# Fewer identity products, and all six tiles turned ahead of the first sums

## The chip, the cores and the metric

The kernel runs on one core of a Trainium2 chip. The metric is the device time of one execution in microseconds (us); lower is better. The time before is 1680.26 us, the median of three runs (1679.79 to 1680.38).

## The reference

Two layers of a diffusion backbone over 512 latent tokens with a prefix of 256 context tokens, model width 1024. Each sub-layer is normalised, shifted and scaled by a modulation that comes from the conditioning vectors `c` (latent tokens) and `c_ctx` (context tokens). The part that matters here is the very beginning of layer 0:

```python
def _rms(x, gain, eps=1e-6):
    xf = x.astype(jnp.float32)
    y = xf * lax.rsqrt(jnp.mean(xf * xf, axis=-1, keepdims=True) + eps)
    return (y * gain.astype(jnp.float32)).astype(x.dtype)
...
sc = jax.nn.silu(c)
scc = jax.nn.silu(c_ctx)
...
m_lat = jnp.split((sc @ mod_w[l] + mod_b[l])[:, None, :], 6, axis=-1)
m_ctx = jnp.split((scc @ mod_w[l] + mod_b[l])[None, None, :], 6, axis=-1)
h_ctx = _modulate(_rms(x_ctx, norm_pre_mix[l]), m_ctx[0], m_ctx[1])
h_lat = _modulate(_rms(x_lat, norm_pre_mix[l]), m_lat[0], m_lat[1])
...
gq, gk, gv, gog, gz, aq, ak, av = _split(h @ w_in, EVEN_SIZES)
```

So 768 token rows are normalised, two of the six parts of the modulation (shift and scale) are matrix products of two vectors with 2048 columns of `mod_w`, and the result `h` goes into the input projection `even_w_in`. All that follows (gated linear attention, attention, feed-forward layers, the second layer) is untouched by the change.

## The kernel before, in words

The tokens are held as six tiles of 128 rows: 0 to 3 latent, 4 and 5 context. The order of work is 4, 5, 0, 1, 2, 3.

The program first runs `constants` (line 377): it builds an identity matrix, issues a number of identity products with `warm(n)` (n products of the identity with itself into a PSUM tile named `idle`, whose result nobody reads; TensorE takes each as two passes), loads the rows of small constants and turns them into columns with one transpose (`pt_rows`, copied to `col`), and from these columns makes `scT`, the activated conditioning vectors.

The first stage stands in `run` (from line 1919). Its steps:

- `fetch` loads the six tiles `xt` on the sync queue, and `loads(qd)` after it loads, quarter by quarter (`qd` 0 to 3), 256 columns of shift and of scale of `mod_w` (tiles `mraw`, nine buffers, two transfers of 256 KB each) and 256 rows of 288 columns of `even_w_in` (`zraw`).
- `turn(t)` normalises and transposes one tile. `mean_rstd` (line 697) squares the tile on ScalarE with a sum over the row (tile `junk`), then GpSimd adds epsilon (line 704) and raises to the power -0.5 (line 705, tile `rs`). VectorE scales the tile by it (line 1956); for the last three tiles this scaling is queued behind a stated earlier copy. TensorE transposes the eight blocks into a PSUM tile of two buffers (`mm_tile`), and a copy to `xT` (line 1961) empties it, on VectorE for the first, second and fifth tile turned, on ScalarE for the others.
- `sums(qd, ks)` multiplies `scT` with the columns of `mod_w`, four narrow products side by side, for the eight blocks of the contraction in two halves (`lo` and `hi`), into `mod_acc`.
- `weights(qd)` splits `zraw` into a rounded part and a remainder: a cast on ScalarE (line 803, `wH`), a difference on GpSimd (line 804, `wL`). It is queued behind the last two copies to `xT`.
- `cols(qd)` copies the sums (`modrows`, line 487), transposes them, adds the bias (`modcol`, line 499) and makes the scale columns `aff` (line 2003) on VectorE.
- `apply(qd, ...)` makes the two parts of `h` from `xT`: ScalarE line 2014, VectorE lines 2015 and 2016.
- `z(t0, qd, ...)` multiplies `h` with the split weights, three products for each block (PSUM tile `nat`).

A loop over the quarters then interleaves the projection of one quarter with the sums of the next. TensorE's instructions carry line 355 (products) and 358 (transposes).

`pin` (line 348) makes an instruction follow, on its own engine, the one traced before it, as long as `self.pinned` is set. All TensorE instructions go through it. The order on the other engines is settled by a planner that lays out the instructions by estimated readiness, unless an `issue_after` block names a predecessor. Semaphores between engines are set from the data.

Of the kernel before, what the change touches and what calls it, by code (L numbers as in the profile page):

```python
# [13 lines left out]
ALU = mybir.AluOpType  # L14
# [13 lines left out]
EPS = 1e-6  # L28
# [288 lines left out]
class Net:  # L317
# [59 lines left out]
    def constants(self):  # L377
        nc, I, cst = self.nc, self.I, self.cst
        self.ident = cst.tile([P, P], F32, name="ident")
        make_identity(nc, self.ident)  # L380
        self.idle = self.sc_tile("idle", 1)[:, :P]
        self.pinned = True
        self.warm(18)
        self.scT = cst.tile([P, KD, 32], F32, name="scT")
        self.neghalf = cst.tile([P, 1], F32, name="neghalf")
        nc.gpsimd.memset(self.neghalf, -0.5)
        self.one = cst.tile([P, 1], F32, name="one")
        nc.gpsimd.memset(self.one, 1.0)

        self.col = cst.tile([P, R_END], F32, name="col")  # L390
        self.modb = self.col[:, R_MB : R_MB + 96]
        self.col_rows(
            "rows", 0, P, (
                (R_C, I["c"].rearrange("o (k p) -> (o k) p", p=P), 8),
                (R_CC, I["c_ctx"].rearrange("(k p) -> k p", p=P), 8),
                (R_NPM, I["norm_pre_mix"].rearrange("l (k p) -> (l k) p", p=P), 16),
                (R_MB, I["mod_b"].rearrange("l (k p) -> (l k) p", p=P), 96),
            )
        )()
        self.pinned = False  # L400

        nc.gpsimd.memset(self.scT, 0.0)
        nc.scalar.activation(
            self.scT[:, :, 0:2].rearrange("p k r -> p r k"),
            self.col[:, R_C : R_C + 16].rearrange("p (r k) -> p r k", r=2),
            AF.Silu,
        )
        self.modcol, self.gates = {}, {}
# [288 lines left out]
    def mean_rstd(self, src):  # L697

        nc = self.nc
        junk = self.wp.tile([P, D], BF16, tag="mraw", bufs=2, name="junk")  # L700
        ms = self.sm.tile([P, 1], F32, tag="ss", name="ss")
        self.squared = nc.scalar.activation(junk, src, AF.Square, scale=1.0 / 32, accum_out=ms)
        rs = self.sm.tile([P, 1], F32, tag="rs1", name="rs")
        nc.gpsimd.tensor_scalar(ms, ms, EPS, None, op0=ALU.add)
        nc.gpsimd.tensor_tensor(rs, ms, self.neghalf, op=ALU.pow)
        return rs

    def pre_norm(self, pool, t, xt, A, B, h, xn):
# [406 lines left out]
    def even_mixer(self, h, mix, z):  # L1115
# [141 lines left out]

        self.pinned = True
        run("qk0 e m qk0 e e v0 qk0 e e m qk0 e e m v0 e e m m q v0 m m v0 m m kv q m q m q m m m m m m m m m m qk1 kv m")
        tp.release()  # L1260
        gp = self.open_pool("gla")
        run("c0 l0 kv m c0 kv c0 v1 qk1 c0 p p qk1 c0 l0 p qk1 l0 c0 g0 qk1 l0 p c1 p v1 l0 p v1 l0 c1 p v1 l0 c1 l1 g1 g0 c1 g0 r0 c1 l1 r0 g0 l1")
        self.tc.keep_in_program_order(nc.scalar.preload_act_table_set("exp_and_others"))
        run("r0 c1 g1 x l1 x g1 l1 x x l1 x l1 x")
        gp.release()
        mg.__exit__(None, None, None)
# [652 lines left out]
    def run(self):  # L1919
        nc, I, out = self.nc, self.I, self.out  # L1920
# [13 lines left out]
        order = (4, 5, 0, 1, 2, 3)  # L1934
# [4 lines left out]
        with self.pool("pre0") as pp:  # L1939
# [10 lines left out]
            def turn(t):  # L1950
                xt = xts.pop(t)
                rs = self.mean_rstd(xt)
                with ExitStack() as behind:
                    if len(emptied) > 2:
                        behind.enter_context(self.tc.issue_after(emptied[min(len(emptied) - 3, 1)].ins))
                    nc.vector.tensor_scalar(xt, xt, rs, None, op0=ALU.mult)
                pt = self.mm_tile(f"xT{t}")
                for k in range(KD):
                    self.tr(pt[:, k * P : (k + 1) * P], xt[:, k * P : (k + 1) * P], self.ident)
                copy = nc.vector.tensor_copy if len(emptied) in (0, 1, 4) else nc.scalar.copy  # L1960
                emptied.append(copy(xT[:, :, t * P : (t + 1) * P], pt.rearrange("p (k i) -> p k i", k=KD)))
# [7 lines left out]
            def loads(qd):  # L1969
                for k in range(0, KD, 2):  # L1970
                    u = pp.tile([P, 2, 2, 256], F32, tag="mraw", bufs=9, name=f"mraw00{qd}{k}")
                    for kk in range(2):
                        nc.sync.dma_start(
                            out=u[:, kk],
                            in_=I["mod_w"][0, (k + kk) * P : (k + kk + 1) * P, 0:2048].rearrange("p (m f) -> p m f", m=2)[
                                :, :, 256 * qd : 256 * qd + 256
                            ],
                        )
                    us[qd, k] = u
                src = w[256 * qd : 256 * qd + 256, 1536 : 1536 + 288].rearrange("(k p) m -> p k m", p=P)  # L1980
                zu.append(self.fetched(src, 2, 288, pp.tile([P, 576], F32, tag="zraw", bufs=4, name="zraw")))

            def sums(qd, ks):
                if ks[0] == 0:
                    accs[qd] = (self.sc_tile("mod_acc", qd) if qd < 2 else self.tr_tile("mod_acc"))[:, :P]
                for k in ks:
                    for j in range(4):
                        self.mm(
                            accs[qd][32 * j : 32 * j + 32, :],
                            self.scT[:, k, :],  # L1990
                            us[qd, k // 2 * 2][:, k % 2, j // 2, (j % 2) * P : (j % 2) * P + P],
                            start=(k == 0),
                            stop=(k == KD - 1),
                            tile_position=(0, 32 * j),
                        )
                if ks[-1] == KD - 1:
                    accs[qd] = self.mod_cols(0, accs[qd], P, [(m, r, 2 * qd, 2 * m, r, 2) for m in range(2) for r in range(2)])

            def cols(qd):
                accs[qd]()  # L2000
                ks = slice(2 * qd, 2 * qd + 2)
                gain = self.col[:, R_NPM + 2 * qd : R_NPM + 2 * qd + 2]
                nc.vector.scalar_tensor_tensor(
                    A[:, :, ks], self.mod_m(0, 1)[:, :, ks], 1.0, gain[:, None, :].to_broadcast([P, 2, 2]), op0=ALU.add, op1=ALU.mult
                )

            def apply(qd, r, t0, n):
                tok = slice(t0 * P, (t0 + n) * P)
                for k in range(2 * qd, 2 * qd + 2):
                    H, L = h.hl(k, tok)  # L2010
                    a, b = A[:, r, k : k + 1], B[:, r, k : k + 1]
                    x = xT[:, k, tok]
                    f = pp.tile([P, SEQ], F32, tag="xa", bufs=4, name="xa")[:, : n * P]
                    cast = nc.scalar.activation(H, x, AF.Identity, bias=b, scale=a)
                    nc.vector.tensor_scalar(f, x, a, b, op0=ALU.mult, op1=ALU.add)
                    self.mark = nc.vector.tensor_tensor(L, f, H.bitcast(F32), op=ALU.subtract)
                    self.latest = cast, self.mark

            def weights(qd):
                with self.behind():  # L2020
                    zu[qd] = zu[qd](vector=nc.gpsimd)
# [20 lines left out]
            fetch(*order)  # L2042
            for qd in range(4):
                loads(qd)
            for t, n in zip(order[:-1], (1, 18, 2, 3, 3)):
                turn(t)
                self.warm(n)
            sums(0, lo)
            turn(order[-1])
            self.warm(3)  # L2050
            sums(0, hi)
            self.latest = emptied[5], emptied[4]
            weights(0)
            self.warm(2)
            cols(0)
            self.warm(5)
            apply(0, 1, 4, 2)
            apply(0, 0, 0, 4)
            for qd in range(1, 4):
# [227 lines left out]
```

## Time and profile before

| | before |
|---|---|
| median of three runs | 1680.26 us |
| the profiled execution, its own time | 1680.16 us |
| its span | 1678.4 us |
| TensorE busy | 1649.9 us (98%) |
| VectorE busy | 1311.4 us (78%) |
| ScalarE busy | 915.6 us (55%) |
| GpSimd busy | 131.5 us (8%) |
| bytes moved by DMA | 204.79 MB |

PE is TensorE, PEld its weight loads, DVE is VectorE, ACT is ScalarE, POOL is GpSimd, SPq the sync engine's queue of transfers and ACTq ScalarE's. A row in order of time gives the start in us, the duration in us, the engine, the source line, the operation, what it writes and reads, the shapes, the number of merged instructions, and in brackets the idle time of the engine before it with what ended it. The chain of work is followed back from the last instruction, so that its rows add up to the span. In the rows of windows the last three columns are granted TensorE clock, DMA share and GB/s, and each engine has its busy time with the number of instructions. A transfer's row gives KB each and the median time from issue to landing.

### The profile page before, as it was taken

The numbers are of one execution on the slowest core, as the hardware profiler recorded it, in microseconds if no ns is written. First come the engines' busy times: TensorE is split into PE (matmuls) and PEld (weight loads), VectorE is DVE, ScalarE is ACT, GpSimd is POOL, SyncE is SP. The second block draws the span as 40 slices with busy tenths as digits, with TensorE's granted clock in tenths as the row PEclk, the third lists the DMA queues.
The fourth block names the chain that finished last, engine by engine and source line by source line (L and its number), as shares of the span: only waits on it lengthen the run. The fifth ranks groups of instructions, "written<-read, shape, count | busy, mean of one in ns | idle before, by whom it ended". The sixth has DMA issues, their size and how long they took to land.

```text
span 1678.4 us, 32622 instructions
## 1 busy us (share of the span) xinstructions
PE 1649.9 (98%) x13457; PEld 1486.4 (89%) x13457; DVE 1311.4 (78%) x2097; ACT 915.6 (55%) x1551; POOL 131.5 (8%) x139
## 2 busy tenths in 40 slices
PE   9999998999999999999999999999999999999998
PEld 8898987888999999998887788888888899999886
DVE  4889768876898989778668648778775599987887
ACT  4645557845544443445447536566564565555564
POOL 2004110001000000002101000000000100000310
PEclk9999999999999999999999999999999999999999
DMA  9651002164243446249516542111115334433973
GB/s 339 187 154 41 3 27 101 52 201 155 86 149 101 139 146 192 77 136 222 101 60 208 191 131 64 52 53 50 52 54 161 125 107 120 115 101 102 221 168 138
DMA packets 184736, 204.79 MB, mean 122 GB/s; under 512 B 7142, under 2 KB 141836, under 8 KB 184588
## 3 DMA queue, kind: packets, MB, share of 16 engines
q1 hardware_dynamic: 173996, 181.98, 34.7%
q0 software_dynamic: 9024, 17.30, 5.9%
q10 hardware_dynamic: 1568, 3.43, 0.6%
q8 instruction: 105, 1.72, 0.4%
q14 instruction: 43, 0.35, 0.1%
HBM read 193.23 MB, written 9.46 MB: 121 GB/s over the span
## 4 chain that ended last, share of the span: by engine, by line
PE 83%; DVE 8%; ACT 3%; DMA 3%; issue 2%; POOL 0%; DVEq 0%; SPq 0%; ACTq 0%; POOLq 0%
PE nat L355 12%; PE a L355 10%; PE ff L355 8%; PE E L355 7%; PE oproj L355 6%; PE x L355 6%; PE o L355 4%; PE D L355 4%; PE b L355 4%; PE fq L355 3%; PE gqk L355 2%; PE pearly L355 2%; PE q L355 2%; PE S L355 2%; PE poh L355 1%
## 5 line engine op out<-in xcount | busy, mean ns | idle before, releaser
L355 PE MATMUL nat<-wH,x 128*128 128x256 f32 (+2 forms) x968 | 226.8, 322 | 1.3 <-issue 0.5
L860 ACT CAST wH<-raw 128x1024 fp32r<-128x1024 f32 x120 | 124.9, 1051 | 101.8 <-DVE raw L885 38.4
L355 PEld LDWEIGHTS nat<-wH,x 128*128 128x128 f32 x968 | 162.0, 190 | 19.1 <-ACT natq L1196 1.7
L861 DVE TENSOR_TENSOR wL<-raw,wH 128x1024 fp32r<-128x1024 f32 x120 | 145.8, 1222 | 23.8 <-ACT wH L860 23.3
L355 PE MATMUL nat<-wL,x 128*128 128x256 f32 (+2 forms) x484 | 153.6, 317 | 1.8 <-DVE wL L804 1.8
L804 DVE TENSOR_TENSOR wL<-raw,wH 128x1024 fp32r<-128x1024 f32 x79 | 95.8, 1223 | 49.6 <-ACT wH L803 48.6
L355 PE MATMUL ff<-x,wH 128*128 128x512 f32 (+1 forms) x512 | 127.7, 341 | 0.0
L686 POOL TENSOR_TENSOR rs<-ms,neghalf 128x1 f32<-128x1 f32 (+2 forms) x56 | 60.2, 1079 | 777.8 <-DVE ms L684 777.7
L803 ACT CAST wH<-raw 128x1024 fp32r<-128x1024 f32 x79 | 82.2, 1050 | 68.3 <-PE ff L355 19.4
L355 PE MATMUL oproj<-wH,x 128*128 128x512 f32 x320 | 102.2, 395 | 0.4 <-ACT x L1330 0.4
L355 PEld LDWEIGHTS nat<-wL,x 128*128 128x128 f32 x484 | 92.1, 190 | 8.4 <-DVE wL L804 2.7
L615 DVE SCALAR_TENSOR_TENSOR macc<-mraw,scT,macc 128x1024 f32<-128x1024 f32 x70 | 88.1, 1282 | 10.4 <-DMA mraw<-in_mod_w_dram 10.2
L355 PEld LDWEIGHTS ff<-x,wH 128*128 128x128 f32 x512 | 87.3, 190 | 10.0
L1773 POOL DMA_DIRECT2D t<-in_ffn_w_down_dram x36 | 41.9, 1200 | 639.7 <-DVE t L1812 337.9
L355 PE MATMUL x<-wH,two 128*128 128x512 f32 x280 | 90.7, 393 | 0.9 <-DVE y L1851 0.7
L1012 ACT COPY qkh<-arr 128x512 f32<-128x512 f32 x112 | 70.4, 643 | 36.8 <-DVE arr L1017 32.3
L355 PE MATMUL ff<-x,wL 128*128 128x256 f32 (+1 forms) x256 | 86.2, 337 | 0.0
L885 DVE TENSOR_TENSOR raw<-raw 128x512 f32<-128x512 f32 x120 | 82.8, 690 | 2.8
L1017 DVE TENSOR_TENSOR arr<-arr,f 128x512 f32<-128x512 f32 x112 | 74.4, 688 | 2.2 <-ACT qkh L1012 0.3
L355 PEld LDWEIGHTS oproj<-wH,x 128*128 128x128 f32 x320 | 60.0, 188 | 12.9 <-ACT x L1330 0.9
L355 PE MATMUL E<-T,wH 128*128 128x384 f32 (+1 forms) x320 | 70.4, 309 | 0.6 <-DVE go L938 0.6
L355 PE MATMUL a<-T,wH 128*128 128x384 f32 (+1 forms) x320 | 70.6, 309 | 0.1
(425 smaller groups left out, 4572.0 us busy)
## 6 DMA issues: line engine op xcount, KB each, us to landing
mraw<-in_mod_w_dram SPq DMA_DIRECT2D x80, 512.0 KB, 4.4
raw<-in_ffn_w_gate_dram SPq DMA_DIRECT2D x44, 512.0 KB, 3.8
raw<-in_ffn_w_up_dram SPq DMA_DIRECT2D x44, 512.0 KB, 4.7
raw<-in_odd_w_in_dram SPq DMA_DIRECT2D x40, 512.0 KB, 3.7
t<-in_ffn_w_down_dram POOLq DMA_DIRECT2D x30, 512.0 KB, 8.6
raw<-in_ffn_w_down_dram SPq DMA_DIRECT2D x28, 512.0 KB, 7.5
mraw<-in_mod_w_dram SPq DMA_DIRECT2D x32, 256.0 KB, 6.1
raw<-in_even_w_in_dram SPq DMA_DIRECT2D x16, 512.0 KB, 5.0
```

Of the source, the lines that this page charges most:

```text
L355: return self.pin(self.nc.tensor.matmul(*a, **k))
L615: nc.vector.scalar_tensor_tensor(a, u, w, a, op0=ALU.mult, op1=ALU.add)
L686: nc.gpsimd.tensor_tensor(rs, ms, self.neghalf.to_broadcast([P, w]), op=ALU.pow)
L803: self.casts = self.casts[-1:] + [nc.scalar.copy(H[:, :m], raw[:, :m])]
L804: vector.tensor_tensor(L[:, :m], raw[:, :m], H[:, :m].bitcast(F32), op=ALU.subtract)
L860: self.nc.scalar.copy(H, f)
L861: self.nc.vector.tensor_tensor(L, f, H.bitcast(F32), op=ALU.subtract)
L885: add = lambda o, x, y: nc.vector.tensor_tensor(o, x, y, op=ALU.add)
L1012: nc.scalar.copy(qkv[:, :, :, half, :], dst)
L1017: nc.vector.tensor_tensor(dst, dst, tb, op=ALU.mult)
L1773: add = lambda o, src: self.pin(nc.gpsimd.dma_start(out=o, in_=src, accum_op=ALU.add))
```

## The change

Identity products are taken away in seven places (18 to 16 in `constants`; in the first stage from 1, 18, 2, 3, 3, 3, 2 and 5 to 0, 5, 1, 1, 1, 2, 1 and 3). The turn of the sixth tile, which stood between the two halves of the first sums, now stands ahead of both. The two GpSimd steps of `mean_rstd` are pinned, so that they follow each other tile by tile in the order in which the program states them.

```diff
@@ -380,7 +380,7 @@
         make_identity(nc, self.ident)
         self.idle = self.sc_tile("idle", 1)[:, :P]
         self.pinned = True
-        self.warm(18)
+        self.warm(16)
         self.scT = cst.tile([P, KD, 32], F32, name="scT")
@@ -701,8 +701,8 @@
         ms = self.sm.tile([P, 1], F32, tag="ss", name="ss")
         self.squared = nc.scalar.activation(junk, src, AF.Square, scale=1.0 / 32, accum_out=ms)
         rs = self.sm.tile([P, 1], F32, tag="rs1", name="rs")
-        nc.gpsimd.tensor_scalar(ms, ms, EPS, None, op0=ALU.add)
-        nc.gpsimd.tensor_tensor(rs, ms, self.neghalf, op=ALU.pow)
+        self.pin(nc.gpsimd.tensor_scalar(ms, ms, EPS, None, op0=ALU.add))
+        self.pin(nc.gpsimd.tensor_tensor(rs, ms, self.neghalf, op=ALU.pow))
         return rs
@@ -2042,18 +2042,16 @@
             fetch(*order)
             for qd in range(4):
                 loads(qd)
-            for t, n in zip(order[:-1], (1, 18, 2, 3, 3)):
+            for t, n in zip(order, (0, 5, 1, 1, 1, 2)):
                 turn(t)
                 self.warm(n)
             sums(0, lo)
-            turn(order[-1])
-            self.warm(3)
             sums(0, hi)
             self.latest = emptied[5], emptied[4]
             weights(0)
-            self.warm(2)
+            self.warm(1)
             cols(0)
-            self.warm(5)
+            self.warm(3)
             apply(0, 1, 4, 2)
             apply(0, 0, 0, 4)
```

## The prediction

> **What bounds the kernel now.** I read the page first, then the chain of work over the first 90 us, then the order of time engine by engine, then the transfers.
>
> ```profile
> span 1678.4 us, 32622 instructions
> ...
> PE 83%; DVE 8%; ACT 3%; DMA 3%; issue 2%; POOL 0%; DVEq 0%; SPq 0%; ACTq 0%; POOLq 0%
> ```
>
> The program is a TensorE chain. What is gained in the first stage reaches the end if nothing behind it waits for the clock on the wall, such as a transfer that has not moved. The chain of that stage:
>
> ```profile
> 8.76 1.09 PE xT L358 x8
> 9.85 0.22 PE idle L355 x2
> 10.08 0.87 PE xT L358 x8
> 10.95 4.02 PE idle L355 x36
> ...
> 15.84 0.45 PE idle L355 x4
> ...
> 17.16 0.67 PE idle L355 x6
> ...
> 18.71 0.67 PE idle L355 x6
> ...
> 21.41 0.67 PE idle L355 x6
> 22.08 1.01 PE mod_acc L355 x32
> ...
> 29.69 1.01 PE mod_acc L355 x32
> ```
>
> "idle" is the identity product of `warm`: two passes each, 36 passes in 4.02 us, 0.112 us a pass. Between tile 4 and the second half of the first sums, 0.22 + 4.02 + 0.45 + 3 x 0.67 = 6.70 us of the chain are such products. What would hold TensorE without them is seen on the other engines (first GpSimd, then ScalarE, VectorE, TensorE):
>
> ```profile
> 5.73 0.23 POOL L704 TENSOR_SCALAR ss<-ss 128x1 f32<-128x1 f32 x1 [4.16 <-ACT junk L702]
> 7.06 0.21 POOL L704 TENSOR_SCALAR ss<-ss 128x1 f32<-128x1 f32 x1 [1.11 <-ACT junk L702]
> 7.35 1.39 POOL L705 TENSOR_TENSOR rs<-ss,neghalf 128x1 f32<-128x1 f32 x2
> 8.83 0.78 POOL L704 TENSOR_SCALAR ss<-ss 128x1 f32<-128x1 f32 x1
> 9.69 0.57 POOL L705 TENSOR_TENSOR rs<-ss,neghalf 128x1 f32<-128x1 f32 x1
> ```
>
> ```profile
> 8.22 0.19 ACT L702 ACTIVATION_READ_ACCUMULATOR junk<-xt 128x1 f32 x1
> ...
> 15.88 1.01 ACT L1961 COPY xT<-xT 128x1024 f32<-128x1024 f32 x1 [3.35 <-PE xT L358]
> ```
>
> ```profile
> 7.95 1.58 DVE L1956 TENSOR_SCALAR xt<-xt,rs 128x1024 f32<-128x1024 f32 x2 [7.95 <-POOL rs L705]
> 10.29 0.75 DVE L1956 TENSOR_SCALAR xt<-xt,rs 128x1024 f32<-128x1024 f32 x1 [0.76 <-POOL rs L705]
> ...
> 11.16 2.35 DVE L1961 COPY xT<-xT 128x1024 f32<-128x1024 f32 x2
> 13.42 2.07 DVE L1956 TENSOR_SCALAR xt<-xt,rs 128x1024 f32<-128x1024 f32 x3
> ```
>
> ```profile
> 1.62 3.78 PE L355 MATMUL idle<-ident 128*128 128x128 f32 x16 [1.62 <-POOL ident masks.py:199]
> ```
>
> ```profile
> 7.88 0.30 PE L358 MATMUL pt_rows<-ident,rows 128*128 128x128 f32 x1
> ```
>
> ```profile
> 19.31 1.08 PE L355 MATMUL mod_acc<-mraw,scT 128*32 128x128 f32 x32
> ...
> 22.01 1.08 PE L355 MATMUL mod_acc<-mraw,scT 128*32 128x128 f32 x32
> ```
>
> GpSimd added the constant for tile 5 (7.06) before it raised tile 4 to its power (7.35). The add of tile 0 took 0.78 instead of 0.21 to 0.23: it ended at 9.61, just behind VectorE's scaling of tile 5 (9.53). So a small GpSimd step that meets a scaling waits for its end.
>
> **The change, part by part.** *Two products less at the start.* Four passes, 0.45 us, end earlier; worth nothing, because the transpose of the constant rows behind them waits for its last transfer:
>
> ```profile
> 2.06 0.44 ACTq L414 DMA_DIRECT2D rows<-in_mod_b_dram  x1
> ...
> rows<-in_mod_b_dram ACTq DMA_DIRECT2D x1, 48.0 KB, 5.7
> ```
>
> 2.06 + 5.7 = 7.76, and the transpose begins at 7.88. It stays there, and tile 4's transposes cannot begin before about 8.0.
>
> *GpSimd's pairs kept together.* Tile 4's power starts at 5.73 + 0.23 + 0.08 = 6.04 and ends at 6.62 (0.57 each), its scaling runs 6.64 to 7.40, and the transposes go at 8.0 instead of 8.76: 0.7 us. Queued behind that power is now tile 5's add (7.06): it meets the scaling and ends near 7.48; power to 8.14, scaling 8.16 to 8.92. Tile 0: sum of squares ready at 8.41, add held to 9.00, power to 9.65, scaling from 9.67 instead of 10.29. No transfer moves: SyncE's loads are issued ahead and wait for landings.
>
> *Fewer products and the new order.* I take VectorE's order as in the rows above (scaling 0, constants, copies of tiles 4 and 5, scalings 1 to 3), all 0.62 us earlier: copies 10.54 to 11.76 and to 12.89, scalings ending 13.55, 14.2, 14.87. The products fall from 30 to 10 between tile 4 and the second half of the sums, and VectorE becomes the limit. Tile 5's transposes start at 8.97, five products end at 10.96. Tile 0 waits for the PSUM buffer of tile 4, 11.81, and ends at 12.74 (8 x 0.109 and a start of 0.06); one product, 12.96. Tile 1 waits for its scaling: 13.60 to 14.53; product, 14.75. Tile 2 goes at once (tile 0's buffer is copied out by ScalarE in 1.01, to about 13.95): to 15.63; product, 15.85. Tile 3 waits for tile 1's copy, 15.75, so not at all: to 16.73. Two products, 17.18. Then both halves of the sums without a gap: first half 17.27, second 18.17 instead of 22.01. By this order **3.84 us** are gained up to the second half's start.
>
> *Do the weights of the sums land in time?* Rows of the sync queue, of its waits between 17 and 20 us, and of the tile's landings between 10 and 24 us:
>
> ```profile
> 5.76 5.77 SPq L1973 DMA_DIRECT2D mraw<-in_mod_w_dram  x8
> ```
>
> ```profile
> 19.15 0.37 SPq L1973 DMA_DIRECT2D mraw<-in_mod_w_dram  x1
> ```
>
> ```profile
> SPq L1973 <- DMA zraw<-in_even_w_in_dram: 1.2, 1, 1.2
> ```
>
> ```profile
> DMA to landing us min/median/max: 5.9/6.6/7.2
> ```
>
> The first quarter's last issue starts at 11.16 and lands between 17.1 and 18.4; its products come in the last part of the second half, after 18.6. Second quarter: last issue 19.15, landed at the latest at 26.4, wanted at 29.69 - 3.8 = 25.9 and later, with the median (25.8) in time. Later ones have more room.
>
> *What is late next: the projection's first weights.* The 1.2 us wait that ends at 19.15 is for `zraw` of quarter 0: it lands only then. Now its cast comes after ScalarE's last copy at 22.36, well behind that. After the change ScalarE is free at 17.95 and waits for the landing.
>
> ```profile
> 22.36 0.68 ACT L803 CAST wH<-zraw 128x576 fp32r<-128x576 f32 x1
> ```
>
> ```profile
> 23.11 1.41 POOL L804 TENSOR_TENSOR wL<-zraw,wH 128x576 fp32r<-128x576 f32 x1 [8.90 <-ACT wH L803]
> ```
>
> ```profile
> 23.16 0.29 DVE L487 COPY modrows<-mod_acc 128x128 f32<-128x128 f32 x1 [3.19 <-PE mod_acc L355]
> ...
> 24.27 0.26 DVE L2003 SCALAR_TENSOR_TENSOR aff<-modcol,col 128x4 f32<-128x4 f32 x1
> ...
> 32.24 0.17 DVE L2003 SCALAR_TENSOR_TENSOR aff<-modcol,col 128x4 f32<-128x4 f32 x1
> ```
>
> Cast from 19.17, GpSimd's difference 0.75 later as now, 19.92 to 21.33. VectorE's `aff` would be due at 24.27 - 3.84 = 20.43, inside that difference. In quarter 0 now it also meets the end of the difference (24.52), takes 0.26 instead of 0.17 and ends at 24.53; so it was held for 0.09. I take it that it is held again, to 21.35: **3.18 us** before 24.53, and all that follows (`apply`, the projection) hangs on it. Bounds for the hold: none (gain 3.84, the difference being in time for the second product of the projection), or the whole rest of the difference (3.18); I take the second, because the one row that shows the meeting ends with the difference.
>
> [...]
>
> *One and two products less around `cols`.* Nothing: the transpose there waits for `modrows` (23.16 + 0.29), and the projection for `aff` and `apply`. Were the second group longer than that chain, each would cost 0.22.
>
> *Behind the stage.* The weights of the next stage land with much room:
>
> ```profile
> 44.00:47.00 3.00, 3.00 (x59) 2.44 (x52) 0.29 (x1) 0.00 (x0) 1.59 (x2) 1.00 0.03 5
> ```
>
> In this stretch the DMA share is 0.03: the queue has run dry, and the next transfers wait for buffers, which come earlier too. So the gain should pass through.
>
> **Sum.** 3.18 of 1680.16 (the profiled execution; 0.1 under the median) gives 1676.98, or **1677.1** against the median of 1680.26. This is minus 0.19%, and 0.2% (3.4 us) is about what a measurement of this kernel can tell from no change.
>
> **Rivals.** (1) `aff` is not held, or the first weights land before 18.4: the TensorE order alone counts, 3.84, 1676.4. For it: only 0.09 us of holding has been seen. A VectorE that copies tile 4 before it scales tile 0 would add up to 0.8 (it idles 0.76 before 10.29), 1675.6. (2) VectorE's order turns out worse than I took it: one copy out of PSUM behind one scaling more delays tile 0 or 1 by 0.66 or 1.2; 2.0 to 2.6 gained, 1677.7 to 1678.3. For it: its order is the planner's, only three scalings have a stated predecessor. (3) The planner orders later work otherwise, since the first stage ends earlier in its count. One difference of 1.4 us or copy of 1.2 us put wrongly costs as much; two or three would take the gain away: 1677 to 1681. Against it: what follows moves as a block. (4) Slower: TensorE falls back to its slow pace for want of identity products. At the start 16 passes take 3.78 us, some 0.22 apart, against 0.11 later. From tile 4 to the end of the sums there are 48 transposes, 20 passes and 16 groups of sums, 84 slots at 0.11 more: 9.2 lost, 3.2 gained, 1686.3. It decides from 29 slow slots on (60 for 0.2% slower). Against it: between the row transpose at 7.88 and 8.76 TensorE had nothing to do and went on at 0.11 (eight transposes in 0.87); the longest gap I foresee is 0.85 (10.96 to 11.81). [...]
>
> **How the numbers follow.** Forecast as summed, gain 2.9 to 3.5: 0.44, of which about a quarter lies beyond 0.2%. Rival 1: 0.27. Rival 2: 0.13. Rival 3: 0.10, a third of it outside on the fast side. Rival 4: 0.06. Faster by over 0.2%: 0.10 + 0.27 + 0.03 = 0.40; slower 0.06 + 0.01 = 0.07; the rest 0.53. From 1675.4 (rival 1 with the copy first) to 1679.2 (rival 2 and the better part of rival 3) lie some 0.85; the forecast's own range is 1676.7 to 1677.4.
>
> **What would show it.** In the profile after: tile 4's scaling near 6.6 and its transposes at 8.0; the add of tile 5 stretched to end behind that scaling; a chain with about 2.2 us of "idle" products and new waits of `xT` for VectorE; the second half of the sums at 18.2; the cast of quarter 0 starting at the landing, 19.2; `aff` stretched by about 0.9 and ending with GpSimd's difference at 21.35; everything from the first `apply` on 3.2 us earlier. Wrong would be: `aff` at its 0.17 inside the difference; sums beginning after 18; passes 0.22 apart behind 8 us; or a first stage that ends 3 us earlier while the span doesn't.

## The result

| | before | after |
|---|---|---|
| median (8 runs each) | 1679.76 us | 1674.76 us |
| lowest to highest | 1678.39 to 1680.38 | 1674.12 to 1675.78 |
| the profiled execution, its own time | 1680.16 us | 1675.78 us |
| its span | 1678.4 us | 1674.0 us |

The ratio is 0.9971, with a 95% interval of 0.996 to 0.9982: 5.0 us or 0.29% faster, outside the range of the prediction by 0.64 us. Of this 0.5 us is the kernel before itself, whose median here is 1679.76 and was 1680.26 when the range was stated. The forecast was a gain of 3.18 us.

The page after: the program is the same TensorE chain.

```profile
span 1674.0 us, 32524 instructions
...
PE 83%; DVE 8%; ACT 3%; DMA 3%; issue 2%; POOL 0%; SPq 0%; DVEq 0%; ACTq 0%; POOLq 0%
```

The chain of work over the first 60 us, first of the kernel after, then the one row of before that it is measured by. `PE nat L355 x31` is the same run of products of the last quarter in both.

```profile
13.89 1.06 PE xT L358 x8
...
17.15 0.45 PE idle L355 x4
17.59 1.88 PE mod_acc L355 x64
19.48 0.42 PE idle L355 x2
...
20.65 0.17 DVE aff L2003
...
46.38 4.46 PE nat L355 x31
```

```profile
50.06 4.45 PE nat L355 x31
```

50.06 - 46.38 = 3.68 us are gained by then. This difference is called the *early gain* below; `aff` ends at 20.82 instead of 24.53, and that is already all of it (3.71). Both halves of the sums run as 64 products in one go, and the identity products have shrunk to what is quoted and two rows of 0.22.

The stage in order of time, in the kernel after: GpSimd, VectorE, TensorE, ScalarE.

```profile
5.91 0.23 POOL L704 TENSOR_SCALAR ss<-ss 128x1 f32<-128x1 f32 x1 [4.34 <-ACT junk L702]
6.23 0.57 POOL L705 TENSOR_TENSOR rs<-ss,neghalf 128x1 f32<-128x1 f32 x1
7.26 0.40 POOL L704 TENSOR_SCALAR ss<-ss 128x1 f32<-128x1 f32 x1 [0.47 <-ACT junk L702]
...
18.85 1.41 POOL L804 TENSOR_TENSOR wL<-zraw,wH 128x576 fp32r<-128x576 f32 x1 [5.07 <-ACT wH L803]
```

```profile
6.83 0.75 DVE L1956 TENSOR_SCALAR xt<-xt,rs 128x1024 f32<-128x1024 f32 x1 [6.83 <-POOL rs L705]
...
9.86 0.75 DVE L1956 TENSOR_SCALAR xt<-xt,rs 128x1024 f32<-128x1024 f32 x1 [0.76 <-POOL rs L705]
...
12.99 2.07 DVE L1956 TENSOR_SCALAR xt<-xt,rs 128x1024 f32<-128x1024 f32 x3
...
20.65 0.17 DVE L2003 SCALAR_TENSOR_TENSOR aff<-modcol,col 128x4 f32<-128x4 f32 x1
```

```profile
8.01 2.24 PE L358 MATMUL xT<-ident,xt 128*128 128x128 f32 x16
...
12.00 1.09 PE L358 MATMUL xT<-ident,xt 128*128 128x128 f32 x8 [0.63 <-DVE xT L1961]
```

```profile
17.18 1.01 ACT L1961 COPY xT<-xT 128x1024 f32<-128x1024 f32 x1 [1.19 <-PE xT L358]
18.09 0.68 ACT L803 CAST wH<-zraw 128x576 fp32r<-128x576 f32 x1
```

The add of tile 5 (7.26) takes 0.40 and ends at 7.66, just behind VectorE's scaling (7.58), as foreseen. The surprise is at 18.09: the cast of the first weights follows the copy with no wait for a landing, GpSimd's difference is over by 20.26, and `aff` at 20.65 has its usual 0.17.

The second part of the gain lies far behind the stage. Two rows of before, TensorE in order of time:

```profile
161.78 0.25 PE L355 MATMUL pcg<-qkg 64*32 64x32 f32 x4 [0.56 <-issue]
...
206.27 0.28 PE L355 MATMUL nat<-wH,x 128*128 128x256 f32 x1 [0.46 <-issue]
```

There TensorE stands still and waits for nothing that the profile shows; the kernel after has no such wait between 150 and 210 us. Aligned by the same TensorE instruction, the lead of the kernel after is 3.71 us at the projection, 4.33 behind the first place and 4.94 behind the second, so each was worth 0.6. From there to the last instruction of TensorE it drifts to 4.4. That drift means nothing: two executions of the unchanged kernel before drift against each other too, from 0.24 at 215 us to 2.1 at the end. The median gain of 5.0 is about 3.7 and 1.2.

### The profile page after: what moved, and what is told of

It is laid out like the page before. It is cut to its first block, busy times and chain, and to the rows that moved or that the text cites. A ratio compares the mean times of both kernels' runs of the same rounds, so it can differ in the third digit from the quotient of the medians.

```text
span 1674.0 us, 32524 instructions
## 1 busy us (share of the span) xinstructions
PE 1644.8 (98%) x13407; PEld 1481.1 (88%) x13407; DVE 1311.1 (78%) x2097; ACT 916.1 (55%) x1551; POOL 129.4 (8%) x139
## 3 DMA queue, kind: packets, MB, share of 16 engines
q8 instruction: 105, 1.72, 0.4%
## 4 chain that ended last, share of the span: by engine, by line
PE 83%; DVE 8%; ACT 3%; DMA 3%; issue 2%; POOL 0%; SPq 0%; DVEq 0%; ACTq 0%; POOLq 0%
PE nat L355 12%; PE a L355 10%; PE ff L355 8%; PE E L355 7%; PE oproj L355 6%; PE x L355 6%; PE o L355 5%; PE D L355 4%; PE b L355 3%; PE fq L355 3%; PE gqk L355 2%; PE pearly L355 2%; PE q L355 2%; PE S L355 2%; PE poh L355 1%
## 5 line engine op out<-in xcount | busy, mean ns | idle before, releaser
L355 PE MATMUL nat<-wH,x 128*128 128x256 f32 (+2 forms) x968 | 226.7, 322 | 1.2 <-ACT x L2014 0.6
L355 PEld LDWEIGHTS nat<-wH,x 128*128 128x128 f32 x968 | 161.9, 190 | 19.5 <-ACT natq L1196 1.7
L355 PE MATMUL nat<-wL,x 128*128 128x256 f32 (+2 forms) x484 | 153.5, 317 | 1.8 <-DVE wL L804 1.8
L355 PE MATMUL ff<-x,wH 128*128 128x512 f32 (+1 forms) x512 | 127.6, 340 | 0.0
L355 PE MATMUL oproj<-wH,x 128*128 128x512 f32 x320 | 102.2, 394 | 0.4 <-ACT x L1330 0.4
L355 PEld LDWEIGHTS nat<-wL,x 128*128 128x128 f32 x484 | 92.1, 190 | 7.8 <-DVE wL L804 2.7
L615 DVE SCALAR_TENSOR_TENSOR macc<-mraw,scT,macc 128x1024 f32<-128x1024 f32 x70 | 88.0, 1282 | 11.6 <-DMA mraw<-in_mod_w_dram 11.4
L355 PEld LDWEIGHTS ff<-x,wH 128*128 128x128 f32 x512 | 87.3, 190 | 10.0
L355 PE MATMUL x<-wH,two 128*128 128x512 f32 x280 | 90.5, 392 | 0.9 <-DVE y L1851 0.7
L355 PE MATMUL ff<-x,wL 128*128 128x256 f32 (+1 forms) x256 | 86.2, 337 | 0.0
L355 PEld LDWEIGHTS oproj<-wH,x 128*128 128x128 f32 x320 | 59.9, 188 | 13.0 <-ACT x L1330 1.0
L355 PE MATMUL a<-T,wH 128*128 128x384 f32 (+1 forms) x320 | 70.5, 309 | 0.6 <-ACT qb L923 0.5
L355 PE MATMUL E<-T,wH 128*128 128x384 f32 (+1 forms) x320 | 70.4, 309 | 0.7 <-DVE go L938 0.7
```

The source lines that it names most:

```text
L355: return self.pin(self.nc.tensor.matmul(*a, **k))
L615: nc.vector.scalar_tensor_tensor(a, u, w, a, op0=ALU.mult, op1=ALU.add)
```

## The experiments

There are two questions: why the first weights were in time though the trace of before had them land at 19.15, and what the stalls at 161 and 206 us have to do with a change in the first 25 us. The early gain of each kernel is 50.06 less the start of its `PE nat L355 x31`; the lead at 215 us is against the same TensorE instruction in the trace of before.

| kernel | early gain | lead at 215 us | time of the one execution |
|---|---|---|---|
| `after` | 3.68 | 4.94 | 1675.78 |
| `after_again` (unchanged) | 3.96 | 5.28 | 1673.75 |
| `before_again` (unchanged) | -0.04 | 0.24 | 1678.01 |
| `late_cast` | 1.96 | 3.33 | 1678.29 |
| `long_early` | 1.50 | 2.27 | 1677.76 |
| `long_late` | 3.68 | 4.69 | 1675.23 |
| `short_before` | -0.14 | 1.13 | 1678.10 |
| `early_warm` | 2.96 | 4.08 | 1674.98 |
| `copy_first_warm` | 4.07 | 5.46 | 1674.18 |
| `pin_only` | 0.68 | 1.47 | 1677.25 |
| `no_pin` | 3.07 | 4.37 | 1674.59 |
| `order_back` | 3.20 | 4.42 | 1675.31 |
| `counts_back` | 0.86 | 2.28 | 1679.26 |

**The two kernels again.** First how much one execution tells.

> The kernel before, unchanged, executed and profiled once more. Theory 'ends of the fetched blocks': the stalls of TensorE at 161.8 (0.78 us from one product to the next) and at 206.3 (0.74) come back in the same places, lead 0 all along, span 1678.2 to 1678.6. Rival 'each execution has its own stalls': one or both are missing, a lead of 0.6 to 1.3 grows behind them without any change, span 1677.1 to 1677.8.

> The changed kernel, unchanged, executed and profiled once more. Theory 'first block': fetch at about 19, zraw of quarter 0 landed at about 18.1, aff at 0.17 us, lead 3.7 at the projection. If instead the clock falls to 0.5 in the first stage, as with the late cast, the lead is about 2.2 there: the gap of 0.61 us ahead of the projection would be near the limit. Later leads 4.3 and 4.9 if the ends of the blocks decide; anything between 3.5 and 5 if each execution has its own stalls.

The early gain repeats within 0.3 (3.96: the load of tile 0 landed at 7.14 instead of 7.63, and its scaling began at 9.59 instead of 9.86). The stall in `pcg` came again in before (0.6 us), the one in `nat` with 0.2 instead of 0.5; the kernel after had neither again. Times of single executions differ by 2 us with no change, so the two columns in the middle are what the experiments are read by.

**Is `aff` held, if the difference comes late?** One more copy on ScalarE ahead of the first cast, on the kernel after:

```diff
+            late = pp.tile([P, D], BF16, name="late")
+            with self.behind():
+                again = nc.scalar.copy(late.rearrange("p (k i) -> p k i", k=KD), xT[:, :, 3 * P : 4 * P])
+            self.latest = again, emptied[4]
             weights(0)
```

> The changed kernel with one more copy of 128x1024 on ScalarE (its output is read by nobody) between its last copy to xT and the cast of quarter 0. It moves the cast, and with it GpSimd's difference, about 1.0 us later: 19.1 and 19.85 to 21.3 us instead of 18.09 and 18.85 to 20.25. Theory 'aff is held by the difference': aff, due at 20.65, takes about 0.7 us instead of 0.17 and ends with the difference at 21.3; the first product of the projection moves from 21.51 to about 22.1, and the lead over the kernel before at the projection falls from 3.7 to about 3.1 us. Rival 'no hold': aff stays at 0.17 us, first product at 21.5, lead 3.7.

GpSimd and VectorE in order of time, and the windows of 3.41 us around the first projection (after the span of the window: busy us and instructions of TensorE, its weight loads, VectorE, ScalarE and GpSimd; then granted clock, DMA share and GB/s):

```profile
19.64 1.40 POOL L804 TENSOR_TENSOR wL<-zraw,wH 128x576 fp32r<-128x576 f32 x1 [5.48 <-ACT wH L803]
```

```profile
20.36 0.69 DVE L2003 SCALAR_TENSOR_TENSOR aff<-modcol,col 128x4 f32<-128x4 f32 x1
```

```profile
20.43:23.84 3.41, 2.15 (x13) 1.56 (x12) 3.37 (x8) 2.51 (x4) 0.61 (x1) 1.00 1.10 353
23.84:27.25 3.41, 3.41 (x39) 2.65 (x38) 0.77 (x2) 0.67 (x1) 0.61 (x1) 0.50 1.10 354
```

The hold is there: `aff` takes 0.69 instead of 0.17 and ends at 21.05, 0.01 behind the difference. But the hold costs 0.5 us, and the early gain fell by 2.0 against `after_again`, which this execution follows until 20.36. The other 1.5 are in the second row of the windows: for 3.41 us the granted clock was 0.50. The second quarter's sums took 1.87 us, not 1.01, as the chain of work shows:

```profile
24.40 1.87 PE mod_acc L355 x32
...
48.10 4.45 PE nat L355 x31
```

None of the theories had that in its number.

**What makes the weights land earlier or later?** The kernel after with 25 tiny products (32 columns, two passes each), as many as the change took out of TensorE's stream (55 identity products before, 30 after, fewer in nine places): in `constants`, behind `self.warm(16)`, where TensorE waits anyhow (`long_early`), or behind the three products that follow `cols(0)` (`long_late`). The stream up to the first cast is then as long as before, or as short as after.

```diff
+    def tiny(self, n):
+        for i in range(n):
+            j = i % 4
+            self.mm(self.idle[32 * j : 32 * j + 32, :32], self.ident[:, :32], self.ident[:, :32],
+                    start=True, stop=True, tile_position=(0, 32 * j))
...
         self.warm(16)
+        self.tiny(25)
```

> The changed kernel with 25 tiny products (32x32 outputs that nobody reads) right after the first 16 identity products, where TensorE waits for the last constant row anyway. TensorE's stream of instructions then is as long as before the change, and the extra part comes early. Theory 'the first block of TensorE's instructions, fetched by DMA, delays the weights of quarter 0': the first fetch comes at 13 to 16.5 us instead of 19.14, zraw of quarter 0 lands at about 19.1 instead of 18.07, the cast starts at 19.2, and if aff is held by the difference it ends at 21.35: lead at the first projection 3.0 to 3.2 us. Rival 'zraw landed early for another reason, or by chance': cast at 18.1, lead 3.7. Theory on the later gain, 'the ends of the fetched blocks decide where TensorE runs out of instructions': the lead does not grow at 157 and 201 us of the kernel before; span 1675.0 to 1675.6. Rival 'the later gain comes from the earlier start': lead grows by 1.2 behind 157 us as in the changed kernel.

> The changed kernel with 25 tiny products (32x32, read by nobody) behind the three identity products that follow the first modulation columns, where TensorE waits 0.6 us for ScalarE. The stream of instructions is as long as before the change from there on, and unchanged ahead of it. Theory 'first block': fetch at about 19 us and cast at 18.1 as in the changed kernel, first projection 0 to 0.2 us later than there, lead 3.5 to 3.7. Theory 'ends of the fetched blocks': the wait of TensorE for nothing shown ahead of pcg (0.56 us at 161.78 before) and the stall of 0.74 at 206 are back, the lead stays 3.5 to 3.7 behind 157 and 201 us; span 1674.6 to 1675.0. Rival 'the later gain comes from the earlier start': the lead grows to 4.3 and 4.9 as in the changed kernel.

`long_early`, ScalarE, GpSimd and VectorE (its lines stand ten further down):

```profile
19.33 0.67 ACT L813 CAST wH<-zraw 128x576 fp32r<-128x576 f32 x1 [1.13 <-DMA zraw<-in_even_w_in_dram]
```

```profile
20.08 1.40 POOL L814 TENSOR_TENSOR wL<-zraw,wH 128x576 fp32r<-128x576 f32 x1 [5.64 <-ACT wH L813]
```

```profile
20.66 0.84 DVE L2013 SCALAR_TENSOR_TENSOR aff<-modcol,col 128x4 f32<-128x4 f32 x1
```

`long_late`, ScalarE:

```profile
18.12 0.67 ACT L812 CAST wH<-zraw 128x576 fp32r<-128x576 f32 x1
```

The very course of the prediction, brought back by 25 products that hinder nobody: the cast waits 1.13 us for `zraw`, the difference runs from 20.08 to 21.48, `aff` is held to 21.50. With the same products eleven microseconds later, nothing of it. What moves is a fetch of instructions by DMA. The list of DMA queues shows it (queue and kind: packets, MB, share of the 16 engines): in `long_early` between 10 and 18.5 us, in before between 16 and 18 us, and in the kernel after not before 18.5 to 20.5 us.

```profile
q8 instruction: 1, 0.02, 0.9%
```

```profile
q8 instruction: 1, 0.02, 3.5%
```

```profile
q8 instruction: 1, 0.02, 3.6%
```

3.5% of 16 engines for 2 us is 1.1 us of one engine. In before the fetch starts at 16.41; of the sixteen parts of quarter 0's `zraw` fifteen have landed by 17.89 and the last at 19.14, 1.25 us behind. That the late part went by the engine of the fetch is inferred from this: the traces do not name the engines. In `long_early` the fetch starts at 12.67 and `zraw` lands at 19.31; in `long_late` they are 19.12 and 18.10. It holds over all fourteen traces: with the fetch starting between 11.4 and 16.6 us `zraw` landed at 19.1 to 19.4 (before, `before_again`, `long_early`, `early_warm`, `pin_only`, `counts_back`), with the fetch from 18 us on at 17.9 to 18.1 (the others). The order of the loads is no rival for this: the sync queue issues everything up to this `zraw`, and the eight loads behind it, in the same order in all fourteen. On the page of the kernel after q8 has 105 fetches and 1.72 MB, 16.4 KB each, and TensorE has 2 x 13407 instructions, 255 for each fetch. That these are TensorE's instructions is inferred: `long_early` and `long_late` differ in the place of TensorE's 25 products alone. So the change, by taking 50 passes with their weight loads out of the stream, moved the fetch from 16.41 to 19.14, behind the landing (18.07).

**Why 1.5 us more?** `long_early` lost 2.18 of the early gain: 0.68 by the hold, the rest again by the clock. Windows of it:

```profile
20.71:24.12 3.41, 1.99 (x12) 1.39 (x11) 3.37 (x8) 2.51 (x4) 0.77 (x1) 1.00 1.10 354
24.12:27.53 3.41, 3.41 (x40) 2.65 (x39) 0.94 (x2) 0.67 (x1) 0.63 (x1) 0.50 1.09 353
```

In both kernels TensorE waits longer than in the kernel after (0.61) ahead of its first projection product: 1.14 in `late_cast`, 1.29 in `long_early`. If that is the cause, then `long_early` with eight identity products instead of three behind `cols(0)` must keep the clock and have the hold:

```diff
             cols(0)
-            self.warm(3)
+            self.warm(8)
```

> The changed kernel with the 25 tiny products behind the first 16 identity products (first block of instructions fetched early, zraw of quarter 0 late), and now eight identity products instead of three behind the first modulation columns, so that the gap of 1.29 us that TensorE had there is filled to about 0.2. Theory 'TensorE's slow pace came from that gap': no stretch with a granted clock of 0.5, the second sums take 1.08 us instead of 1.94, and only the hold of aff is left: lead over the kernel before at the projection 2.9 to 3.1 us. Rival 'the lead was lost to late weights': sums stay at 1.94, lead 1.5.

VectorE in order of time, a window, and the chain:

```profile
20.46 1.11 DVE L2013 SCALAR_TENSOR_TENSOR aff<-modcol,col 128x4 f32<-128x4 f32 x1
```

```profile
20.80:24.21 3.41, 2.84 (x20) 2.24 (x19) 3.37 (x8) 2.50 (x4) 0.74 (x1) 1.00 1.10 358
```

```profile
24.72 1.01 PE mod_acc L355 x32
...
47.10 4.47 PE nat L355 x31
```

The hold is the longest seen (1.11), the wait of TensorE is 0.44, the clock stays at 1.00, the sums take 1.01, and the early gain is 2.96: `aff` ends at 21.57, and 24.53 - 21.57 = 2.96. Hold and clock are two things, and this execution has the first alone. It is one execution, and it shows that the products cover the fall here; a longer wait elsewhere left the clock alone (last section).

**The stalls at 161 and 206 us.** The kernel before with a stream shorter by the same 25 products, without being earlier: where many identity products stand, one of 512 columns takes the place of four.

```diff
+    def wide(self, n):
+        out = self.idle4.rearrange("p (a b) -> p a b", a=4)
+        for _ in range(n):
+            self.mm(out, self.ident, self.ident[:, None, :].to_broadcast([P, 4, P]), start=True, stop=True)
...
-        self.warm(18)
+        self.wide(4)
+        self.warm(4)
```

(and likewise the 18 behind tile 5 as `wide(4)` and `warm(2)`, the 5 behind `cols(0)` as `wide(1)` and `warm(1)`)

> The kernel before with 36 of its identity products replaced by 9 that are four times as wide and with two narrow ones more at the start: TensorE's time in the first stage stays the same, its stream is as short as that of the changed kernel. Theory 'ends of the fetched blocks': no lead at the first projection (0 to 0.1 us), then a lead of about 0.7 behind 157 us and 1.2 behind 201 us; span 1677.0 to 1677.8. Rival 'the later gain comes from the earlier start': no lead anywhere, span 1678.2 to 1678.6. Theory 'first block': its fetch comes after 18 us and zraw of quarter 0 lands by 18.2, which nothing waits for here.

Its early gain is -0.14, and yet its lead at 215 us is 1.13: both stalls are gone. The one at 206 goes by the length of the stream: the lead grew there by 0.61 or 0.62 in all eight executions whose stream is shorter than before's (by 25 products in six of them, by 22 in `copy_first_warm` and by 5 in `counts_back`), and by 0.05 to 0.30 in the four with before's length (`early_warm`, five longer, 0.44). The one at 161 does not: it stands in both executions of the kernel before and in no other, and the waits of TensorE between 154 and 209 us in `pin_only`, whose stream is before's, show the second alone.

```profile
PE nat L355 <- issue: 0.4, 1, 0.4
```

**The parts.** The change is three edits. One kernel adds the pins to the kernel before, three take one edit out of the kernel after:

```diff
# pin_only: before, with
+        self.pin(nc.gpsimd.tensor_scalar(ms, ms, EPS, None, op0=ALU.add))
+        self.pin(nc.gpsimd.tensor_tensor(rs, ms, self.neghalf, op=ALU.pow))
# no_pin: after, without these two
# order_back: after, with
+            for t, n in zip(order[:-1], (0, 5, 1, 1, 1)):
...
             sums(0, lo)
+            turn(order[-1])
+            self.warm(2)
             sums(0, hi)
# counts_back: after, with
+            for t, n in zip(order, (1, 18, 2, 3, 3, 3)):
```

> The kernel before with GpSimd's two norm steps pinned and nothing else. The power of tile 4 starts at about 6.1 us and its transposes at 8.0 instead of 8.76; behind that TensorE has its products as before, so the lead over the kernel before is 0.7 at the projection. TensorE's stream of instructions is the same as before, only earlier. Theory 'ends of the fetched blocks': the stalls at 161.8 and 206 stay, the lead is 0.7 to 1.0 behind them, span 1677.3 to 1677.8. Rival 'the later gain comes from the earlier start': the lead grows to 1.4 behind the first and to 2 behind the second.

> The changed kernel with GpSimd's two steps not pinned. The scaling of tile 4 is at 8.0 again, its transposes at 8.76, VectorE's copies and scalings 0.5 to 0.6 later than in the changed kernel, and with them tiles 0 and 1 and the sums: lead over the kernel before at the projection 3.1 to 3.3 instead of 3.7.

> The changed kernel with the turn of the sixth tile between the two halves of the first sums again (identity products and pins as changed). By TensorE's order alone the second half of the sums starts 0.1 to 0.2 later, lead 3.5 to 3.6 at the projection. But the copy of the sixth tile, and the cast of quarter 0 behind it, come about 1.0 later on ScalarE: difference 19.9 to 21.3, aff (due at about 20.85) held to 21.3: lead 3.1 to 3.2; and if the gap ahead of the projection brings the clock down to 0.5, 1.7 to 2.0. Rival 'order doesn't matter': lead 3.7.

> The changed kernel with the former identity products between the tiles (1, 18, 2, 3, 3, 3); order and pins as changed. TensorE is busy with them again: 0.7 from the earlier start and 0.1 to 0.3 from the gaps that the old order had around the sixth tile. Lead at the projection 0.8 to 1.1. Rival 'the new order alone brings most': lead over 2.

The chains of the four, in this order:

```profile
49.38 4.47 PE nat L355 x31
```

```profile
46.99 4.45 PE nat L355 x31
```

```profile
20.86 0.49 DVE aff L2003
...
46.86 4.45 PE nat L355 x31
```

```profile
49.20 4.46 PE nat L355 x31
```

The pins are worth 0.68 alone and 0.6 beside the rest (3.68 - 3.07). The fewer products between the tiles (10 instead of 30) are worth 2.8 (3.68 - 0.86). The order is worth 0.5 (3.68 - 3.20): `aff` starts 0.21 later, and since ScalarE's sixth copy, and with it the cast, comes a microsecond later, it is held for 0.31 more. Each of these is one execution; against `after_again` (3.96) they would be 0.9, 3.1 and 0.8.

**A step further.** In the kernel after VectorE stands idle for 0.76 ahead of the scaling of tile 0 (9.86), with tile 4 ready in PSUM. Here the copies of tiles 4 and 5 go ahead of the scaling of tile 0, and six products instead of three stand behind `cols(0)`:

```diff
-                    if len(emptied) > 2:
-                        behind.enter_context(self.tc.issue_after(emptied[min(len(emptied) - 3, 1)].ins))
+                    if len(emptied) > 1:
+                        behind.enter_context(self.tc.issue_after(emptied[min(max(len(emptied) - 3, 0), 1)].ins))
...
-            self.warm(3)
+            self.warm(6)
```

> The changed kernel with VectorE's scaling of the third tile turned queued behind its copy of the first (so that VectorE doesn't stand idle from 9.10 to 9.86), and six identity products instead of three behind the first modulation columns, against a gap there. Tile 0 is turned at about 12.3 instead of 12.0, tile 1 at 13.4 instead of 13.89, the first sums start at 17.1 instead of 17.52. aff is due at about 20.2, where GpSimd's difference ends (20.25). Lead over the kernel before at the projection 4.0 to 4.2 us instead of 3.7; median 0.3 to 0.5 us under the changed kernel's, less than one run tells. Rival: the later copy of tile 5 delays tile 0 by more, lead 3.5 or less.

```profile
12.45 1.06 PE xT L358 x8
...
20.31 0.17 DVE aff L2003
...
45.99 4.47 PE nat L355 x31
```

The early gain is 4.07, a tenth over `after_again`. Timed, the median is 1674.09 us (eight runs, 1672.96 to 1676.16) against 1679.27 for before beside it: a ratio of 0.997, interval 0.996 to 0.9981. That is the ratio of the kernel after; it is not shown to be better.

## Why the prediction was wrong, and where it was right

*The failed step: "`zraw` of quarter 0: it lands only then" (19.15).* The landing was taken from the trace of before as if it were fixed, because no load had moved ("No transfer moves"). But the instruction fetch that by the inference above shares a DMA engine with it had moved, along with TensorE's stream, to 19.14. `zraw` landed by 18.07, which is the second half of rival 1 ("the first weights land before 18.4"). In the sum it stands as 3.18 instead of 3.71: `aff` ended at 20.82 and not at 21.35.

*A term that was not in the sum.* "The gain should pass through" was too little: two stalls of 0.6 us went as well. The trace of before showed them as waits for "issue", but nothing behind 90 us was priced. 3.18 + 0.5 + 1.2 = 4.9, against the 5.0 measured.

*The order on TensorE: right, slightly too high.* 3.84 was forecast up to the second half of the sums. Its end came at 19.47 instead of 23.09 (chain), 3.62 earlier, and in `after_again` at 19.21, 3.88 earlier. The difference is the load of tile 0: its squares ended at 8.87 instead of 8.41, and so the scaling began at 9.86 and not at 9.67. Tile 4's scaling at 6.83 (forecast 6.64), the transposes at 8.01 (8.0) and the wait of tile 0 for the copy of tile 4, to 12.00 (11.81), came as written. VectorE's order was as taken, so rival 2 did not occur; nor did rival 3 cost anything: VectorE, ScalarE, GpSimd and TensorE have their instructions in the order of before from the first quarter's loop on, and on the sync queue one load alone, the last quarter's `zraw`, goes out later (33.9 us instead of 28.9).

*The hold: right in kind and size, only not in this kernel.* It came wherever the difference ran late: 0.69, 0.84, 1.11 and 0.48 instead of 0.17, each time ending within 0.03 of GpSimd. Had the landing been as I took it, `long_early` says that the hold alone would have given 24.53 - 21.50 = 3.03.

*"One and two products less around `cols`. Nothing."* True for this kernel, which has no row for them. But the cover that they gave is gone: in the one execution with the landing and the hold that I forecast, the clock fell (`long_early`, 1.50 us of gain in all), and with eight products it did not (`early_warm`, 2.96). My own forecast had no price for this. Rival 4, the slow pace, was priced for the transposes, by the longest single gap; it came in two of the experiments and not in this kernel, behind the stage, after waits of 1.14 and 1.29 us.

*The chances.* 0.53 stood on a change of no more than 0.2%; it was 0.29%. Rival 1's chance of 0.27 was too small: the one unknown that it hung on, a landing among other transfers, was priced as known.

What stays open: why the stall at 161 us vanishes both for `short_before` (a shorter stream, not earlier) and for `pin_only` (before's stream, 0.7 us earlier). That TensorE waits for instructions in both places was argued from the length of the stream, and for 206 us the executions agree with it; what the stall waits for no trace shows.

## What to carry to other kernels

Instructions cost transfers, here 105 fetches of 16.4 KB. Taking 25 products out of the stream moved the first fetch from 16.41 to 19.14 us; the landing of a load in flight came earlier with it (18.07 instead of 19.14), and one stall far behind the edit went, worth 0.6 us. So a landing read off a trace is no constant, even where no load is touched; ask what else ran on the DMA engines just then, and give the landing a range. And before identity products are thinned out, look at each wait of TensorE that they covered, with the wait as long as the forecast itself makes it, and give a fall of the clock behind it a price: here it was 1.5 us, behind waits of 1.14 and 1.29 us.

## What the hardware showed that I had not expected

- A fetch of 16 KB of instructions, by the inference above TensorE's, took about 1.1 us by the profile (1.12 in before, 1.16 in the kernel after). The DMA share was 1.09 to 1.11 from 14 to 22 us (before and after). Where the fetch started between 11.4 and 16.6 us the load landed at 19.1 to 19.4, where it started from 18 us on at 17.9 to 18.1; in the kernel before one of its sixteen parts landed 1.25 us behind the others (17.89 to 19.14).
- The granted clock fell to 0.50, for 3.41 us, though TensorE had work ahead of the fall. In the 3.41 us ahead of it TensorE was busy for 2.15 (`late_cast`) and 1.99 us (`long_early`) by the profile. With waits of 0.93 (`order_back`) and 0.61 us (the kernel after) at the same place it stayed at 1.00. But neither that busy time nor the wait decides alone. In `late_cast` itself, a later stretch of 3.41 us has less busy time (2.05) and a longer wait of TensorE (1.36 us), and the clock stayed at 1.00 in it and behind it:

```profile
252.53:255.94 3.41, 2.05 (x23) 1.50 (x22) 3.13 (x5) 0.22 (x1) 0.00 (x0) 1.00 0.67 255
```

```profile
254.88 0.66 PE L355 MATMUL attO<-probT,natk 128*64 128x128 f32 x8 [1.36 <-DVE probT L210]
```

What the clock follows stays open, and with it how much cover a wait needs.
